# The inverse transforms of one frequency group of a long convolution: twelve split matmuls against four plain fp32 ones and two VectorE operations

## The chip, the cores and the metric

The kernel runs on one core of a Trainium2 chip. The metric is the device time of one execution in microseconds, median of several runs. The engines are named as in the profile: PE (TensorE matmuls), PEld (TensorE weight loads, which overlap PE), DVE (VectorE), ACT (ScalarE), POOL (GpSimd) and SP (SyncE). Each works through its own instructions strictly in the order in which they stand in its program.

## The reference

An encoder layer is applied to two inputs of 1024 rows by 1024 channels. Each is normalised and projected; one part goes through a Fourier branch, another through a Hyena branch, and both are gated, merged and projected again. What matters here is the Hyena branch, which does two long convolutions per channel, one after the other:

```python
def long_conv(u, kf, d):
    L = u.shape[1]
    uf = jnp.fft.rfft(u, n=2 * L, axis=1)
    y = jnp.fft.irfft(uf * kf[None], n=2 * L, axis=1)[:, :L]
    return y + d * u
...
    z = v.astype(jnp.float32)
    for n, gate in enumerate((x1, x2)):
        z = gate.astype(jnp.float32) * long_conv(z, kf[:, n],
                                                 hyena_d[n].astype(jnp.float32))
```

`v`, `x1` and `x2` are three 1024-channel projections of the input after a convolution of width 3; `kf` is the spectrum of filters that the layer computes from small weights.

## The kernel before

All data are fp32. A matmul of full precision is mostly made from values split in two (`split`, L168): ACT rounds the source to a high part of type fp32r, and DVE (or POOL) subtracts it from the source to get the low part. `mm3` (L372) then does three fp32r matmuls: high by high, high by low, low by high. A few matmuls are done once on plain fp32 operands; in the profile such a call of 128x128 shows as two records.

**Phases.** First the Fourier branch; then `phase_main` (L868), which begins with the filters' spectra (written to DRAM as `d_k`) beside some gate projections; then, in `branches` (L911), the convolutions; then the remaining gates, the two output projections and the last one. The tables for the forward transform (`cfw0`, `cfwd`) are loaded at the start of `phase_main`, the inverse table `cinv` in thirds after the filters' iterations 2, 4 and 6 (L903 to L908) by POOL's queue.

**The convolutions.** `branches` goes through 32 of them: 2 batches, in each 8 channel tiles of 128 channels and 2 orders. One step builds the next convolution's front (`conv_front`, L782: the projection `pin`, transpositions `tph`, and the first stages of the transform as sums and differences in `butterfly`), then the present one's back (`conv_back`, L796), then gates it. A projection is 48 matmuls of 128x512 on PE.

**`conv_back`** goes through four groups of frequencies in the order 0, 2, 1, 3 (`GROUPS`, L147). Group 0 is the real one: frequencies with index 0 and 4 modulo 8, whose inputs are real, so its forward transform (`forward`, L593) is four plain fp32 matmuls of 128x128 with `cfw0`. The others take twelve fp32r matmuls with `cfwd`. Then, for every group alike:

- DVE multiplies the spectrum X in PSUM by the filter's (`t`, 1024 wide, L806) and adds the parts to Y (`y`, 512 wide, L810).
- ACT rounds Y to `yh`, DVE makes `yl` (L813). `y` has one buffer, `yh` and `yl` have two each.
- PE does the inverse transforms: twelve fp32r matmuls `pT`, with the parts of Y as the stationary side and `cinv` as the moving one, 256 columns each (L816 to L833). For group 0 the table of frequency index 4 stands there twice, once negated, so that the four quarters of `pT` come out as sums and differences of the two frequency classes already. `pT` is one of two PSUM buffers of the tag "T", which the transpositions `tph` use in turn with it.
- For group 0 ACT copies `pT` to `T0s` (L839), and for group 2 DVE adds and subtracts its `pT` (`U`, and `V` in place of `T0s`). Groups 1 and 3 are combined likewise (`T1s`, `S`, `D`, `ez`). Further sums give the output `yc`.

The program's order is not written by hand: a scheduler places the instructions of each engine by its own estimate of time, and pools with numbered buffers set what must wait. So a change in one place can move instructions elsewhere on the engine.

Of the kernel before, what the change touches and what calls it, by code (L numbers as in the profile page):

```python
# [9 lines left out]
F32 = mybir.dt.float32  # L10
# [6 lines left out]
P = 128  # L17
# [29 lines left out]
def _tables():  # L47
    t = {}
    s = np.arange(P) + 0.5
    fwd, inv = [], []  # L50
    th = np.zeros((P, 8, 6))
    for pi, (f1, hf) in enumerate(PAIRS):
        f = f1 + 8 * (np.arange(P) + P * hf)
        w = 2 * np.pi * f / 2048
        c, sn = np.cos(np.outer(s, w)), np.sin(np.outer(s, w))
        wt = np.full(P, 1 / 1024.0)
        if f1 == 0:
            sn[:, 0] = np.sin(np.pi * s)
            wt[0] = 1 / 2048.0
        fwd += [c, sn]  # L60
        ci, si = (c * wt).T, (sn * wt).T
        if f1 == 0:
            inv += [ci, -si]
        elif f1 == 4:
            inv += [ci, -ci, -si, si]
        else:
            inv += [-si, ci, si]
        ang = w * 127.5
        ct, st = np.cos(ang), np.sin(ang)
        ct2, st2, cm = ct.copy(), st.copy(), ct.copy()  # L70
        if f1 == 0:
            ct2[0], st2[0], cm[0] = 0.0, -1.0, 0.0
        if f1 in (0, 4):
            th[:, pi] = np.stack([ct, -st, -cm, -st, -ct2, st2], axis=1)
        else:
            th[:, pi] = np.stack([ct, -st, 0 * ct, 0 * ct, st, 0 * ct], axis=1)
    t["c_fw0"] = np.concatenate(fwd[:4], axis=1).astype(np.float32)
    t["c_fwd"] = _hl(np.concatenate(fwd[4:], axis=1))
    t["c_inv"] = _hl(np.concatenate(inv, axis=1))
    t["c_th"] = th.astype(np.float32)  # L80


    ta = np.arange(L // 2)
    tp = np.arange(258)
    tabs = []
    for fn in (np.cos, np.sin):
        for r in range(2):
            w = 2 * np.pi * np.outer(2 * np.arange(256) + r, tp) / L
            tabs += [fn(w[0:P]), fn(w[P:2 * P])]
    t["c_seq"] = _hl(np.concatenate(tabs, axis=1))  # L90

    ae = np.zeros((P, 2, 86))
    for b in range(2):
        for r in (0, 2, 32, 34):
            ae[r + b, b] = 1.0 - 2.0 * (tp[:86] % 2)
    t["c_alt"] = ae.astype(np.float32).reshape(P, 2 * 86)
    c = np.arange(P)
    cg = np.cos(2 * np.pi * np.outer(c, c) / 256) / 512
    sg = np.sin(2 * np.pi * np.outer(c, c) / 256) / 512
    sg[0] = 0.0  # L100
    sg[:, 0] = 0.0
    d0 = np.zeros((P, P))
    d0[:, 0] = (1.0 - 2.0 * (c % 2)) / 512
    t["c_chan"] = _hl(np.concatenate([cg, sg, d0], axis=1))
    xs = np.zeros((P, 2, 2, P))
    for g in range(2):
        for r in (g, 32 + g):
            xs[r, 0, g] = (1.0 - 2.0 * (c % 2)) / 512
            xs[r, 1, g, 0] = 1.0 / 512
    t["c_chx"] = xs.astype(np.float32).reshape(P, 4 * P)  # L110


    f32 = np.float32
    pos = np.arange(L, dtype=f32)
    tn = pos / f32(L - 1)
    bands = np.linspace(1e-4, BANDS - 1, BANDS, dtype=f32)
    ang = (f32(2.0 * math.pi) * pos / f32(L))[:, None] * bands[None]
    z = np.concatenate([tn[:, None], np.cos(ang), -np.sin(ang)], axis=-1).astype(f32)
    order = []
    for m in range(4):  # L120
        order.append(256 * m + 128 + np.arange(P))
        order.append(256 * m + 127 - np.arange(P))
    order = np.concatenate(order)
    t["c_z"] = np.ascontiguousarray(z[order].T)
    v = np.zeros((P, 14), f32)
    v[:, 0:8] = -tn[order].reshape(8, P).T
    v[:, 8] = 1.0
    v[127, 8] = 0.0
    v[127, 9] = 1.0
    v[1:, 10] = -1.0  # L130
    v[1:, 11] = 1.0
    v[:, 12] = -1.0
    v[0, 12] = 1.0
    t["c_vec"] = v
    t["c_id"] = np.eye(P, dtype=f32)
    return t
# [5 lines left out]
_o = 0  # L142
for _pi, (_f1, _hf) in enumerate(PAIRS):
    IOFF[_pi] = _o
    _o += 256 if _f1 == 0 else (512 if _f1 == 4 else 384)
INVW = _o
GROUPS = [(0, (0, 1)), (2, (4, 5)), (1, (2, 3)), (3, (6, 7))]  # L147
KOFF = {0: 0, 1: 8, 2: 16, 3: 24}
# [13 lines left out]
class K:  # L162
# [633 lines left out]
    def conv_back(self, n, ct, B, ws):  # L796
        nc = self.nc
        ci = self.cinv
        T = {}
        for g, pairs in GROUPS:  # L800
            X = self.forward(g, pairs, B[g], "pX")
            kt = ws.tile([P, 8, P], F32, tag="k", name="k", bufs=2)
            o = KOFF[g] * P
            nc.sync.dma_start(kt.rearrange("p a b -> p (a b)"), self.d_k[n][ct][:, o:o + 8 * P])
            t = ws.tile([P, 2, 2, 2, P], F32, tag="t1", name="t", bufs=1)
            self.mul("dve", t.rearrange("p k h r c -> p k (h r c)"),  # L806
                     X.rearrange("p h r c -> p (h r c)").unsqueeze(1).to_broadcast([P, 2, 512]),
                     kt.rearrange("p (k a) b -> p k (a b)", k=2))
            Y = ws.tile([P, 2, 2, P], F32, tag="y", name="y", bufs=1)
            self.add("dve", Y, t[:, 0], t[:, 1, :, ::-1])  # L810
            yh = ws.tile([P, 2, 2, P], F32R, tag="yh", name="yh", bufs=2)
            yl = ws.tile([P, 2, 2, P], F32R, tag="yl", name="yl", bufs=2)
            self.split(yh, yl, Y, "dve", "act")  # L813
            Tp = self.psum("T", 2, "pT")
            T4 = Tp.rearrange("p (q c) -> p q c", q=4)
            for r in range(2):  # L816
                for i, pr in enumerate(pairs):
                    w = (yh[:, i, r], yl[:, i, r])
                    o = IOFF[pr]
                    if g == 0:  # L820
                        out = T4[:, r::2]
                        if i == 0:
                            R = [ci[:, hl, o + r * P:o + r * P + P].unsqueeze(1).to_broadcast([P, 2, P]) for hl in range(2)]
                        else:
                            R = [ci[:, hl, o + r * 256:o + r * 256 + 256].rearrange("p (a b) -> p a b", a=2)
                                 for hl in range(2)]
                    elif r == 0:
                        out = T4[:, 0::3]
                        R = [ci[:, hl, o + P:o + 3 * P].rearrange("p (a b) -> p a b", a=2) for hl in range(2)]
                    else:  # L830
                        out = T4[:, 1:3]
                        R = [ci[:, hl, o:o + 2 * P].rearrange("p (a b) -> p a b", a=2) for hl in range(2)]
                    self.ended = self.mm3(out, w, R, i == 0, i == 1)  # L833

            def tt(name):
                return ws.tile([P, 512], F32, tag="tt", name=name, bufs=4)
            if g in (0, 1):
                T[g] = tt(f"T{g}s")
                nc.scalar.copy(T[g], Tp)  # L839
            elif g == 3:  # L840
                S_, D_ = tt("S"), T[1]
                self.add("dve", S_, T[1], Tp)
                self.sub("dve", D_, T[1], Tp)
                ez = ws.tile([P, 2, 256], F32, tag="ez", name="ez", bufs=1)
                self.sub("dve", ez[:, 0], D_[:, 0:256], S_[:, 256:512])
                self.add("dve", ez[:, 1], D_[:, 0:256], S_[:, 256:512])
            else:
                U, V = tt("U"), T[0]
                self.add("dve", U, T[0], Tp)
                self.sub("dve", V, T[0], Tp)  # L850
        q = ws.tile([P, 4, 2, P], F32, tag="q", name="q", bufs=2)
        qf = q.rearrange("p n e s -> p n (e s)")
        self.add("dve", qf[:, 0], U[:, 0:256], S_[:, 0:256])
        self.sub("dve", qf[:, 2], V[:, 0:256], D_[:, 256:512])
        self.stt("dve", qf[:, 1], ez[:, 0], C8, V[:, 256:512])
        self.stt("dve", qf[:, 3], ez[:, 1], -C8, U[:, 256:512])
        y = ws.tile([P, 4, 256], F32, tag="q", name="yc", bufs=2)
        self.add("dve", y[:, :, P:2 * P], q[:, :, 0], q[:, :, 1])
        self.sub("dve", y[:, :, P - 1::-1], q[:, :, 0], q[:, :, 1])
        return y.rearrange("p n s -> p (n s)")  # L860
# [7 lines left out]
    def phase_main(self, nct=8, nb=NB, nf=16):  # L868
        tc, nc, a = self.tc, self.nc, self.a
        with ExitStack() as es:  # L870
# [24 lines left out]
            for i in range(nf):  # L895
# [6 lines left out]
                    self.spill_gate(0, sec, c, ws)  # L902
                if i == 2:  # L903
                    self.cinv = mi.tile([P, 2, INVW], F32R, name="cinv")
                if i in (2, 4, 6):

                    s = slice((2, 4, 6).index(i) * INVW // 3, ((2, 4, 6).index(i) + 1) * INVW // 3)
                    nc.gpsimd.dma_start(self.cinv[:, :, s], a["c_inv"][:, :, s])  # L908
# [560 lines left out]
```

## Time and profile before

| | |
|---|---|
| Median of 3 runs | 2442.94 us (2442.49 to 2445.35) |
| The profiled execution | 2444.67 us |
| Its span, first to last instruction | 2442.9 us |
| Filters and gates ahead of the convolutions | up to about 700 us |
| Convolutions (first and last start of pT) | 731.9 to 1681.3 us |
| PE's mean granted clock | 0.996 |

The profile is of one execution. A line of a group ends in the busy time, the mean duration in ns, and the idle time of the engine ahead of these instructions with what ended it. PE's records overlap: a matmul's record lasts longer than the distance to the next, so what a matmul costs is read from the distance of starts. Tiles are named without buffer numbers; L194 is `mm`, through which nearly all matmuls go, and L181 is `tt`, through which the sums, differences and products on DVE and POOL go, so groups are told apart by their tiles.

### The profile page before, as it was taken

What the parts mean: (1) busy time and instruction counts of PE and PEld (TensorE: products, weight loads), DVE (VectorE), ACT (ScalarE), POOL (GpSimd) and SP (SyncE); (2) the same over time, 40 slices, a digit from 0 to 9 for tenths busy, and PEclk for the clock granted to TensorE, in tenths of its full rate; (3) what the DMA queues carried; (4) which work ended last, traced back from release to release, by engine and by line L of the source; (5) the groups of instructions that cost most, each with busy time, mean ns of one, the idle gap of its engine ahead of it and who ended that gap; (6) DMA issues with size and microseconds to landing.
All of it is one profiled execution on the core that took longest, in us unless ns stands there. A gap on an engine that the chain in (4) does not pass through costs nothing.

```text
span 2442.9 us, 36854 instructions
## 1 busy us (share of the span) xinstructions
PE 2396.8 (98%) x13196; PEld 2084.8 (85%) x13196; DVE 1896.5 (78%) x3405; ACT 1096.7 (45%) x2063; POOL 487.0 (20%) x518
## 2 busy tenths in 40 slices
PE   6999999999999999999999999999999999999998
PEld 5988888888888888888888888888788888888886
DVE  7687888888748999999989999766555455665677
ACT  5546577767633433334223323333344444544343
POOL 1341322222143433331000000112200012122111
PEclk9999999999999999999999999999999999999999
DMA  7535655555555555545444444335454567776543
GB/s 265 187 133 198 218 180 169 169 176 166 172 194 178 172 177 173 163 165 195 147 129 133 141 141 139 121 121 184 141 177 167 190 211 254 253 255 217 170 162 130
DMA packets 225823, 429.36 MB, mean 176 GB/s; under 512 B 23574, under 2 KB 87287, under 8 KB 225256
## 3 DMA queue, kind: packets, MB, share of 16 engines
q1 hardware_dynamic: 198444, 333.34, 42.5%
q0 software_dynamic: 27008, 93.65, 11.1%
q8 instruction: 104, 1.70, 0.3%
q14 instruction: 79, 0.65, 0.1%
q10 hardware_dynamic: 188, 0.02, 0.0%
HBM read 290.60 MB, written 136.31 MB: 175 GB/s over the span
## 4 chain that ended last, share of the span: by engine, by line
PE 92%; DMA 2%; DVE 2%; ACT 1%; issue 1%; POOL 1%; SPq 0%; DVEq 0%; ACTq 0%; POOLq 0%
PE pin L194 41%; PE pT L194 7%; PE pg L194 7%; PE pyf L194 7%; PE pyh L194 7%; PE pX L194 7%; PE po L194 6%; PE pXf L194 3%; PE pfv L194 2%; PE pft L194 1%; PE tph L792 1%; PE tpx L194 1%; DMA x<-in_x 1%; DMA wr<-in_w_fo 0%; DMA d_x<-xg 0%
## 5 line engine op out<-in xcount | busy, mean ns | idle before, releaser
L194 PE MATMUL pin<-xh,wl 128*128 128x512 f32 x1472 | 577.7, 392 | 3.3 <-POOL wl L181 3.3
L194 PE MATMUL pin<-xh,wh 128*128 128x512 f32 x1472 | 577.2, 392 | 0.9 <-DMA wh<-d_w 0.9
L194 PE MATMUL pin<-xl,wh 128*128 128x512 f32 x1472 | 576.2, 392 | 0.4 <-DVE xl L181 0.4
L181 POOL TENSOR_TENSOR wl<-wr,wh 128x512 fp32r<-128x512 f32 x136 | 240.8, 1772 | 1141.9 <-ACT wh L171 1108.1
L171 ACT CAST wh<-wr 128x512 fp32r<-128x512 f32 x264 | 163.5, 620 | 365.0 <-PE pin L194 141.3
L194 PEld LDWEIGHTS pin<-xh,wl 128*128 128x128 f32 x1472 | 277.5, 189 | 55.8 <-POOL wl L181 4.8
L194 PEld LDWEIGHTS pin<-xh,wh 128*128 128x128 f32 x1472 | 277.4, 188 | 52.5 <-DMA wh<-d_w 1.3
L194 PEld LDWEIGHTS pin<-xl,wh 128*128 128x128 f32 x1472 | 277.5, 189 | 52.2 <-DVE xl L181 1.0
L194 PE MATMUL pT<-cinv,yh 128*128 128x256 f32 x1024 | 193.1, 283 | 0.0
L194 PEld LDWEIGHTS pT<-cinv,yh 128*128 128x128 f32 x1024 | 164.0, 190 | 9.0
L181 DVE TENSOR_TENSOR t<-pX,k 128x1024 f32<-128x1024 f32 x128 | 155.7, 1216 | 11.0 <-PE pX L194 9.3
L181 DVE TENSOR_TENSOR wl<-wr,wh 128x512 fp32r<-128x512 f32 x128 | 87.8, 687 | 94.1 <-ACT wh L171 93.8
L194 PE MATMUL pX<-bh,cfwd 128*128 128x256 f32 x768 | 159.6, 286 | 0.0
L194 PE MATMUL pyf<-sf,wh 128*128 128x512 f32 x512 | 157.7, 389 | 0.0
L194 PE MATMUL pyh<-sh,wh 128*128 128x512 f32 x512 | 157.3, 389 | 0.0
L171 ACT CAST bh<-b 128x512 fp32r<-128x512 f32 x144 | 89.0, 620 | 126.0 <-DVE b L181 84.2
L194 PE MATMUL pT<-cinv,yl 128*128 128x256 f32 x512 | 144.9, 283 | 0.0
L171 ACT CAST yh<-y 128x512 fp32r<-128x512 f32 x128 | 79.2, 618 | 112.3 <-DVE y L181 89.5
L194 PEld LDWEIGHTS pX<-bh,cfwd 128*128 128x128 f32 x768 | 126.4, 190 | 2.5
L194 PEld LDWEIGHTS pyh<-sh,wh 128*128 128x128 f32 x512 | 96.1, 188 | 19.9
L194 PEld LDWEIGHTS pyf<-sf,wh 128*128 128x128 f32 x512 | 96.1, 188 | 19.9
L194 PE MATMUL pX<-bl,cfwd 128*128 128x256 f32 x384 | 109.6, 285 | 0.0
(354 smaller groups left out, 5262.9 us busy)
## 6 DMA issues: line engine op xcount, KB each, us to landing
k<-d_k SPq DMA_DIRECT2D x128, 512.0 KB, 4.0
wr<-in_w_in SPq DMA_DIRECT2D x136, 256.0 KB, 3.1
d_g<-gt SPq DMA_DIRECT2D x124, 256.0 KB, 2.8
d_k<-kt SPq DMA_DIRECT2D x128, 128.0 KB, 2.1
d_k<-kt SPq DMA_DIRECT2D x64, 256.0 KB, 2.3
wr<-in_w_fo POOLq DMA_DIRECT2D x64, 256.0 KB, 4.1
g<-d_g SPq DMA_DIRECT2D x64, 256.0 KB, 4.4
wr<-in_w_ho POOLq DMA_DIRECT2D x64, 256.0 KB, 4.0
```

Of the source, the lines that this page charges most:

```text
L171: self.rounded = nc.scalar.copy(h, src)
L181: return e.tensor_tensor(out, a, b, op=op)
L194: return self.nc.tensor.matmul(out, lhsT, rhs, start=start, stop=stop, skip_group_check=shared)
L792: nc.tensor.transpose(tp[:, q * P:(q + 1) * P], eo[:, e, q], self.ident)
```

## The change

Group 0 alone is treated in a way of its own. The inverse tables of its two frequency classes leave `c_inv` (which shrinks from 3072 to 2304 columns per part) and form a table `c_in0` of 512 fp32 columns: cosine and negative sine of class 0, then of class 4, each once. It is loaded by SP's queue after the filters' iteration 2. In `conv_back`, Y of group 0 is not split: it goes unrounded into four plain fp32 matmuls of 128x128, one per class and part, whose results fill the four quarters of a PSUM buffer `pT0`. ACT copies the right half (class 4) to the right half of `T0s`; DVE adds the left half of `pT0` and that copy into the left half of `T0s`, then puts their difference into the right half. Y of group 0 lies in one of the two `yl` buffers and not in the single `y` one. From group 2 on all is as before.

```diff
@@ _tables
-        if f1 == 0:
-            inv += [ci, -si]
-        elif f1 == 4:
-            inv += [ci, -ci, -si, si]
+        if f1 in (0, 4):
+            in0 += [ci, -si]
         else:
             inv += [-si, ci, si]
...
+    t["c_in0"] = np.concatenate(in0, axis=1).astype(np.float32)
...
@@ offsets in c_inv
-    _o += 256 if _f1 == 0 else (512 if _f1 == 4 else 384)
+    _o += 0 if _f1 in (0, 4) else 384
...
@@ conv_back
-            Y = ws.tile([P, 2, 2, P], F32, tag="y", name="y", bufs=1)
+            Y = ws.tile([P, 2, 2, P], F32, tag="y" if g else "yl", name="y" if g else "y0", bufs=1 if g else 2)
             self.add("dve", Y, t[:, 0], t[:, 1, :, ::-1])
+            if g == 0:
+
+                Tp = self.psum("T", 2, "pT0")
+                for i in range(2):
+                    for r in range(2):
+                        s = slice((2 * i + r) * P, (2 * i + r + 1) * P)
+                        self.mm(Tp[:, s], Y[:, i, r], self.cin0[:, s], True, True)
+                T[0] = ws.tile([P, 512], F32, tag="tt", name="T0s", bufs=4)
+                lo, hi = T[0][:, 0:256], T[0][:, 256:512]
+                nc.scalar.copy(hi, Tp[:, 256:512])
+                self.add("dve", lo, Tp[:, 0:256], hi)
+                self.sub("dve", hi, Tp[:, 0:256], hi)
+                continue
...
-                    if g == 0:
-                        out = T4[:, r::2]
-                        if i == 0:
-                            R = [ci[:, hl, o + r * P:o + r * P + P].unsqueeze(1).to_broadcast([P, 2, P]) for hl in range(2)]
-                        else:
-                            R = [ci[:, hl, o + r * 256:o + r * 256 + 256].rearrange("p (a b) -> p a b", a=2)
-                                 for hl in range(2)]
-                    elif r == 0:
+                    if r == 0:
...
-            if g in (0, 1):
-                T[g] = tt(f"T{g}s")
+            if g == 1:
+                T[g] = tt("T1s")
                 nc.scalar.copy(T[g], Tp)
...
@@ phase_main
                     self.cinv = mi.tile([P, 2, INVW], F32R, name="cinv")
+                    self.cin0 = mi.tile([P, 4 * P], F32, name="cin0")
+                    nc.sync.dma_start(self.cin0, a["c_in0"])
```

More of the change, by code (lines that the diff above doesn't have):

```diff
@@ L49, in _tables @@
     s = np.arange(P) + 0.5
-    fwd, inv = [], []
+    fwd, in0, inv = [], [], []
     th = np.zeros((P, 8, 6))
```

## The prediction

> **What bounds the kernel now.** I read the page first, then the stretches of the convolutions, then who waits for whom, then the chain of work, the timeline and the groups. From the page:
>
> ```profile
> PE 2396.8 (98%) x13196; PEld 2084.8 (85%) x13196; DVE 1896.5 (78%) x3405; ACT 1096.7 (45%) x2063; POOL 487.0 (20%) x518
> ...
> PE 92%; DMA 2%; DVE 2%; ACT 1%; issue 1%; POOL 1%; SPq 0%; DVEq 0%; ACTq 0%; POOLq 0%
> PE pin L194 41%; PE pT L194 7%; PE pg L194 7%; PE pyf L194 7%; PE pyh L194 7%; PE pX L194 7%; PE po L194 6%; PE pXf L194 3%; PE pfv L194 2%; PE pft L194 1%; PE tph L792 1%; PE tpx L194 1%; DMA x<-in_x 1%; DMA wr<-in_w_fo 0%; DMA d_x<-xg 0%
> ...
> L194 PE MATMUL pT<-cinv,yh 128*128 128x256 f32 x1024 | 193.1, 283 | 0.0
> ...
> L194 PE MATMUL pT<-cinv,yl 128*128 128x256 f32 x512 | 144.9, 283 | 0.0
> ```
>
> PE is busy for 98% and makes 92% of the chain that ends last; pT, which the change cuts, is 7% of that chain. The 1536 records of pT are 32 convolutions (2 batches, 8 channel tiles, 2 orders) by 4 groups by 12. None of them sat idle (0.0 behind the last bar). Since a busy PE need not be the bound, I look at the stage where these matmuls stand, stretch by stretch (columns: busy us of PE, PEld, DVE, ACT, POOL, each with its count, then PE's granted clock, DMA share and GB/s):
>
> ```profile
> 800.00:900.00 100.00, 100.00 (x608) 89.21 (x607) 98.56 (x151) 38.63 (x70) 36.58 (x36) 1.00 0.54 173
> 900.00:1000.00 100.00, 100.00 (x610) 89.42 (x609) 96.82 (x156) 36.46 (x66) 35.15 (x35) 1.00 0.53 171
> 1000.00:1100.00 100.00, 100.00 (x612) 89.46 (x612) 95.53 (x146) 39.94 (x73) 36.71 (x35) 1.00 0.50 165
> ...
> 1300.00:1400.00 100.00, 100.00 (x606) 89.22 (x605) 94.97 (x157) 31.13 (x56) 0.00 (x0) 1.00 0.45 143
> ...
> 1700.00:1800.00 100.00, 97.01 (x420) 79.48 (x419) 56.52 (x64) 39.67 (x59) 17.60 (x14) 0.98 0.47 157
> ```
>
> and at all that PE waited for from 690 to 1700 us:
>
> ```profile
> PE pin L194 <- DMA wh<-d_w: 0.9, 1, 0.9
> PE pin L194 <- DVE xl L181: 0.4, 1, 0.4
> ```
>
> PE never pauses for a pT, pX or transposition: it is the bound there, at the full clock. The second thing to see is DVE at 95.5 to 98.6% of the first batch's stretches and 95% of the second's: it is the next bound, with 9.1 us free in 300 (300 less 98.56, 96.82 and 95.53). So PE's saving counts in full only as far as DVE can follow.
>
> **PE's part of the change.** Removed per convolution: the twelve fp32r matmuls of the first group. Added: four fp32 ones of 128x128. Starts and not durations give the cost, since matmuls overlap. From the chain of work (start, us, what), then from the timeline, where eight records of the forward transform of the same group are followed by pT, and from the groups:
>
> ```profile
> 720.12 0.88 PE tph L792 x8
> ...
> 737.22 1.44 PE pT L194 x12
> ...
> 755.22 13.63 PE pin L194 x60
> ```
>
> ```profile
> 1005.58 0.98 PEld L194 LDWEIGHTS pX<-b,cfw 128*128 128x128 f32 x8
> ...
> 1006.48 0.30 PEld L194 LDWEIGHTS pT<-cinv,yh 128*128 128x128 f32 x2
> ```
>
> ```profile
> L194 PE MATMUL pX<-b,cfw 128*128 128x128 f32 x256 | 34.8, 274 | 0.0
> ...
> L194 PE MATMUL tpx<-dg,xk 128*128 128x128 f32 x128 | 15.6, 276 | 1.4 <-ACT xg L344 0.9 <-DMA xk<-in_x 0.5
> ```
>
> Twelve pT take 1.44 us, 0.12 each (a pin matmul takes 13.63/60 = 0.227). The forward transform calls four fp32 matmuls of exactly the new shape per convolution, 128 in all, and has 256 records: one call is two records. Eight records take 1006.48 - 1005.58 = 0.90 us of weight loads. In the forward transform the table is the stationary side and the data moves; here it is the other way round. tpx, with its data stationary, has 128 records for 64 calls and the same 276 ns, so the roles do not matter. Saving: 1.44 - 0.90 = 0.54 us per convolution, times 32 = **17.3 us**. The ends: were the eight records as long as their durations (274 ns each, 2.19 us), the convolution would lose 0.75 us; at the group's busy time (34.8/32 = 1.09 us) it would gain 0.35. I take 0.54, as the 0.90 us are a stream with other work on both sides.
>
> [...] In the trace the two kinds load alike, 191 and 190 ns:
>
> ```profile
> L194 PEld LDWEIGHTS pT<-cinv,yh 128*128 128x128 f32 x1024 | 164.0, 190 | 9.0
> ...
> L194 PEld LDWEIGHTS pX<-b,cfw 128*128 128x128 f32 x256 | 33.4, 191 | 1.6
> ```
>
> **DVE's part.** Removed: the subtraction that makes yl for the first group, 512 wide. Added: a sum and a difference, 256 wide each, one operand in PSUM. From the groups by tile (min/median/max in ns), and the timeline:
>
> ```profile
> L171 ACT CAST yh<-y x128: 603/621/627, 729.3 to 1675.7; 128x512 fp32r<-128x512 f32 x128
> L181 DVE TENSOR_TENSOR yl<-y,yh x128: 672/681/1672, 732.8 to 1676.3; 128x512 fp32r<-128x512 f32 x128
> ```
>
> ```profile
> L839 ACT COPY T0s<-pT x32: 578/586/591, 738.9 to 1670.8; 128x512 f32<-128x512 f32 x32
> L181 DVE TENSOR_TENSOR U<-T0s,pT x32: 671/677/689, 740.2 to 1675.5; 128x512 f32<-128x512 f32 x32
> L181 DVE TENSOR_TENSOR q<-U,S x32: 410/418/1069, 755.1 to 1683.2; 128x256 f32<-128x256 f32 x32
> ```
>
> ```profile
> 1000.71 0.75 DVE L181 TENSOR_TENSOR b<-bs 128x256 f32<-128x256 f32 x2
> ...
> 1001.38 0.68 DVE L181 TENSOR_TENSOR y<-t 128x512 f32<-128x512 f32 x1
> ...
> 1007.75 0.68 DVE L181 TENSOR_TENSOR yl<-y,yh 128x512 fp32r<-128x512 f32 x1
> ...
> 1010.56 0.28 PE L194 MATMUL pT<-cinv,yl 128*128 128x256 f32 x1
> ...
> 1010.68 1.28 DVE L181 TENSOR_TENSOR bl<-b,bh 128x512 fp32r<-128x512 f32 x2
> ...
> 1011.88 0.68 DVE L181 TENSOR_TENSOR y<-t 128x512 f32<-128x512 f32 x1
> ```
>
> A PSUM operand costs nothing extra (677 beside 681). In a stream a 256 takes (1001.38 - 1000.71)/2 = 0.335 us and a 512 (1011.88 - 1010.68)/2 = 0.60. So DVE gets 2 x 0.335 - 0.60 = +0.07 us per convolution; without overlap, 2 x 0.418 - 0.60 = +0.24. I take 0.07. DVE's 9.1 us in 300 are 3.0%; a convolution of the first batch takes some 28.2 us (half of the 32.7 us of three projections, 144 x 0.227, plus 48 pT and 36 pX at 0.12, 8 fp32 records and 8 transpositions at 0.11), so DVE has 0.86 us free in each. PE's 0.54 and DVE's 0.07 leave 0.25 us: DVE goes to 99%, but stays below PE. It runs ahead, too: the yl that ends at 1008.43 is used at 1010.56, 2.1 us later.
>
> [...]
>
> **ACT** loses the cast (0.62) and has 256 columns to copy in place of 512; at 39% it is covered. **DMA**: c_inv shrinks by a quarter, c_in0 adds one load of 256 KB on SP's queue during the filters; before the first pT nothing else moves in the program's order.
>
> ```profile
> wr<-in_w_in SPq DMA_DIRECT2D x136, 256.0 KB, 3.1
> ```
>
> A load of that size lands in 3.1 us, hundreds of us before its use: nothing.
>
> **The new waits.** The sum on DVE waits for PE's four matmuls and ACT's copy, and while it waits, everything behind it on DVE waits, with PE behind that. The first group's Y now also lies in the ring of two yl buffers: the yl two further on must wait until the four matmuls have read it. I laid the built program's order beside the paces above. In 28 of 32 convolutions DVE has, between the product of the second group (which releases PE's later transforms) and its first instruction that needs pT0, 4.0 to 7.4 us more work than PE has up to pT0's end; in two it has 2.4 and 0.7 us more, in two (the first ones of the batches) PE has 0.5 and 1.6 us more. So the waits are covered but for about 2 us. The PSUM ring of two: pT0 is held until the difference is done, not just until a copy; up to its next user PE has 6.4 us of other work or more. I cost the waits at 2 us.
>
> **Sum.** The profiled execution took 2444.67 us (span 2442.9). 2444.67 - 17.3 + 2 = 2429.4; the median of the runs is 1.7 us lower, so **2427.6 us**.
>
> **Rivals.**
>
> *DVE becomes the bound.* For it: 95 to 99% busy, in order, and some of its operations already take far longer than their median (yl up to 1672 ns). Against it: its idle time is mostly waiting for PE, which now comes earlier. If DVE can't get below its 0.86 us of idle time, the dozen dense convolutions of the first batch gain nothing and lose the 0.07, and of the second batch half the gain is lost: 17.3 - 12 x 0.61 - 16 x 0.27 = 5.7 us gained; 2437. If only the first batch suffers: 2433.
>
> *The wait for pT0 stops DVE.* Slower than before. Two waits of this kind exist:
>
> ```profile
> DVE S L181 <- PE pT L194: 33.3, 15, 5.8
> ...
> ACT T0s L839 <- PE pT L194: 31.8, 14, 4.4
> ```
>
> They come at about every second convolution, 2.2 us each. The new sum is DVE's version of the second: if DVE stood 2.2 us there in each convolution, behind its 0.25 us of spare time, PE would get its operands 2 us late each time and lose 32 x (2.2 - 0.25 - 0.54) = 45 us net; at every second one, 32 x (1.1 - 0.25 - 0.54) = 10: 2453. It decides from 0.8 us of wait per convolution. Against it: the order above gives DVE 4 us of other work.
>
> *The fp32 matmuls do not run at 0.11 a record.* At the 274 ns of their durations: 2443 + 24 = 2467. Nearly excluded by the 0.90 us.
>
> **Chances.** The forecast (2421 to 2431) 0.62; DVE bound (2431 to 2441) 0.22; DVE stopped by pT0 0.12; fp32 dearer, or order shifts that eat the gain, 0.04. The lower end allows for the 3 us of PE's pauses between 1700 and 1800 us, which may fall otherwise: 2427.6 - 2 (no wait for pT0 at all) - 3 = 2422.6, and 1.6 more for the scatter of the runs (2442.49 to 2445.35). The range 2421 to 2441 leaves out the last two cases and a little below. A measurement of this kernel tells about 0.2% (4.9 us) from no change: faster by more (below 2438) 0.80, within 0.07, slower 0.13.
>
> **What would show it.** PE's group pT falls to 1152 records, pT0 has 256 with no idle time, and eight of its records take 0.9 us. DVE's share between 800 and 1100 us rises to 98 to 99%. If DVE takes over, PE waits for yl, bl or t appear that are absent now; if pT0 stops DVE, there is a wait of the sum for ACT's copy, or of yl for pT0, over 25 us in total. The forecast is wrong if PE's busy share in the convolutions falls below 99%, or if the end shifts without PE's work having shrunk by 17 us.

## The result and the profile after

The changed kernel takes 2427.14 us (median of five runs, 2425.10 to 2428.06) against 2442.94 us (2442.40 to 2445.35): a ratio of 0.9931 with a 95% interval of 0.9918 to 0.9945. The profiled execution took 2428.06 us, its span is 2426.1 us.

First the engines' totals, from the page of the changed kernel, then its matmuls that write pT and what follows them (the view of the tile pT: min/median/max in ns, first and last start):

```profile
PE 2379.7 (98%) x13068; PEld 2066.0 (85%) x13068; DVE 1905.1 (79%) x3437; ACT 1070.9 (44%) x2031; POOL 497.9 (21%) x518
```

```profile
L193 PE MATMUL pT<-cinv,yh x768: 274/283/365, 735.3 to 1667.3; 128*128 128x256 f32 x192
...
L193 PE MATMUL pT<-cinv,yl x384: 274/283/388, 737.0 to 1667.5; 128*128 128x256 f32 x192
...
L193 PE MATMUL pT<-cin,y x256: 270/275/275, 729.5 to 1653.9; 128*128 128x128 f32 x128
L180 DVE TENSOR_TENSOR T0s<-pT,T0s x64: 401/414/424, 731.4 to 1655.1; 128x256 f32<-128x256 f32 x64
```

PE has 13068 records in place of 13196: 384 of pT went (768 + 384 = 1152 are left of 1536) and 256 came, and PE is busy 2396.8 - 2379.7 = 17.1 us less. The span fell by 16.8. So nearly all of PE's saving reached the end.

One of the new groups of eight records, in the timeline of PE:

```profile
932.66 1.05 PE L193 MATMUL pT<-cin,y 128*128 128x128 f32 x8
933.47 0.48 PE L193 MATMUL pT<-cinv,yh 128*128 128x256 f32 x2
933.79 0.28 PE L193 MATMUL pT<-cinv,yl 128*128 128x256 f32 x1
```

From the first of the eight to the next matmul it is 933.47 - 932.66 = 0.81 us; the two yh behind them take 0.32 where two take 0.24 in a stream, so the eight cost 0.81 + 0.08 = 0.89.

The stretches of the convolutions and their end, before and after (columns as in the prediction: busy us and count of PE, PEld, DVE, ACT, POOL, then PE's granted clock, DMA share, GB/s):

```profile
800.00:1100.00 300.00, 300.00 (x1826) 268.09 (x1825) 290.91 (x451) 115.03 (x208) 108.44 (x106) 1.00 0.53 170
1100.00:1200.00 100.00, 98.70 (x568) 85.89 (x567) 93.41 (x144) 36.07 (x58) 7.28 (x4) 1.00 0.51 165
1200.00:1500.00 300.00, 300.00 (x1820) 268.07 (x1820) 277.29 (x449) 91.58 (x162) 0.00 (x0) 1.00 0.44 141
```

```profile
800.00:1100.00 300.00, 298.06 (x1800) 265.11 (x1800) 299.21 (x462) 105.84 (x195) 118.44 (x104) 1.00 0.53 172
1100.00:1200.00 100.00, 98.52 (x551) 85.39 (x550) 88.87 (x144) 33.74 (x55) 9.48 (x4) 0.98 0.51 169
1200.00:1500.00 300.00, 300.00 (x1802) 266.92 (x1802) 276.95 (x458) 83.40 (x151) 0.00 (x0) 1.00 0.44 141
1700.00:1800.00 100.00, 99.01 (x435) 81.25 (x434) 57.92 (x72) 42.05 (x65) 13.24 (x13) 1.00 0.47 161
```

Two things are to be seen. In the first batch's dense stretch DVE is now busy for 299.21 of 300 us, and PE, which never paused there, pauses 1.94 us. And the stretch 1700 to 1800, where PE had 97.01 us and a clock of 0.98, now has 99.01 and 1.00. What PE waited for from 690 to 1700 us, sorted by total (us in total, times, longest):

```profile
PE tph L791 <- DVE T0s L180: 1.2, 2, 0.7
PE pin L193 <- DVE xl L180: 1.0, 1, 1.0
PE pX L193 <- DVE bl L180: 0.6, 1, 0.6
PE pin L193 <- DMA wh<-d_w: 0.2, 1, 0.2
PE pX L193 <- DVE t L180: 0.2, 1, 0.2
```

The new waits are small (tph waits for the PSUM buffer that the difference gives back), 3.2 us in all where there were 1.3. The waits for bl and t, 0.8 us together, are of the kind that the prediction set as a sign of DVE taking over. And from DVE's waits in the same stretch:

```profile
DVE T0s L180 <- ACT T0s L819: 1.9, 2, 1.5
```

The new sum waits for ACT's copy in two of 32 convolutions, for 1.9 us together.

### The profile page after: what moved, and what is told of

The parts are those of the page before. It is cut to its first block, busy times and chain, and to the rows that moved or that the text cites. A ratio compares the mean times of both kernels' runs of the same rounds, so it can differ in the third digit from the quotient of the medians.

```text
span 2426.1 us, 36569 instructions
## 1 busy us (share of the span) xinstructions
PE 2379.7 (98%) x13068; PEld 2066.0 (85%) x13068; DVE 1905.1 (79%) x3437; ACT 1070.9 (44%) x2031; POOL 497.9 (21%) x518
## 4 chain that ended last, share of the span: by engine, by line
PE 48%; DMA 2%; DVE 1%; issue 1%; ACT 0%; POOL 0%; SPq 0%; DVEq 0%; ACTq 0%; POOLq 0%
PE pin L193 14%; PE pyh L193 7%; PE pg L193 7%; PE po L193 6%; PE pyf L193 6%; PE pT L193 4%; PE pX L193 4%; DMA wr<-in_w_fo 1%; DMA xraw<-d_x 1%; PE tph L791 1%; DVE xsum L180 0%; DMA wr<-in_w_in 0%; DMA wraw<-in_w_in 0%; DVE wl L180 0%; DVE xsum L176 0%
## 5 line engine op out<-in xcount | busy, mean ns | idle before, releaser
L180 POOL TENSOR_TENSOR wl<-wr,wh 128x512 fp32r<-128x512 f32 x136 | 254.1, 1869 | 1133.7 <-ACT wh L170 1100.4
L193 PE MATMUL pT<-cinv,yh 128*128 128x256 f32 x768 | 145.6, 284 | 0.0
L193 PEld LDWEIGHTS pT<-cinv,yh 128*128 128x128 f32 x768 | 123.1, 190 | 6.6
L170 ACT CAST yh<-y 128x512 fp32r<-128x512 f32 x96 | 59.5, 619 | 144.7 <-DVE y L180 136.9
L180 DVE TENSOR_TENSOR bl<-b,bh 128x512 fp32r<-128x512 f32 x144 | 104.2, 727 | 7.0 <-ACT bh L170 6.7
```

What stands on the lines that cost most here:

```text
L170: self.rounded = nc.scalar.copy(h, src)
L180: return e.tensor_tensor(out, a, b, op=op)
L193: return self.nc.tensor.matmul(out, lhsT, rhs, start=start, stop=stop, skip_group_check=shared)
```

## The experiments

Two theories stand against each other. **PE**: the gain is PE's own, 17 us of matmuls less, and what DVE and ACT have less or more hardly counts. **DVE**: the gain (or a good part of what is missing in it) is set by DVE, or ACT's relief; then a change of DVE's load moves the end and one of PE's doesn't. A third question is what the buffer of the unsplit Y does.

All changes are against the changed kernel unless another is named. The runs of the kernel before beside them had medians of 2442.70 us (double_table, no_sums, split_once, more_dve), 2441.72 (before_more_dve, one_wide, y_ring, after_again) and 2441.90 (own_y, two_y, before_yl, wide_own).

### PE's work changed alone

**double_table.** Still fp32 and still once, but the table of class 4 stands there twice, once negated, as it did before; the sums come out of PE, and DVE has neither split nor sums for group 0.

```diff
-            in0 += [ci, -si]
+            in0 += [ci, -si] if f1 == 0 else [ci, -ci, -si, si]
...
-                for i in range(2):
-                    for r in range(2):
-                        s = slice((2 * i + r) * P, (2 * i + r + 1) * P)
-                        self.mm(Tp[:, s], Y[:, i, r], self.cin0[:, s], True, True)
+                T4, c0 = Tp.rearrange("p (q c) -> p q c", q=4), self.cin0
+                for r in range(2):
+                    one = c0[:, r * P:(r + 1) * P].unsqueeze(1).to_broadcast([P, 2, P])
+                    two = c0[:, (2 + 2 * r) * P:(4 + 2 * r) * P].rearrange("p (a b) -> p a b", a=2)
+                    self.mm(T4[:, r::2], Y[:, 0, r], one, True, False)
+                    self.mm(T4[:, r::2], Y[:, 1, r], two, False, True)
...
-                nc.scalar.copy(hi, Tp[:, 256:512])
-                self.add("dve", lo, Tp[:, 0:256], hi)
-                self.sub("dve", hi, Tp[:, 0:256], hi)
+                nc.scalar.copy(T[0], Tp)
...
-                    self.cin0 = mi.tile([P, 4 * P], F32, name="cin0")
+                    self.cin0 = mi.tile([P, 6 * P], F32, name="cin0")
```

> The four fp32 matmuls get 256 columns each (class 4's table twice, once negated) and accumulate the sums and differences in PSUM; ACT copies all 512, DVE makes no sum. Against the kernel before, DVE and ACT are relieved more than by the change (DVE by 0.60 us per convolution), PE gets eight records of twice the width: some 1.76 us if a record's time doubles, against 1.44. If PE's time is what was saved: slower than before, about 2443 + 32 x 0.32 = 2453. If the relief of DVE and ACT, or the shorter way without a split, was the gain: 2427 or less.

Measured: 2454.80 us (2454.05 to 2455.76), ratio 1.0053 (1.0038 to 1.0068). Its eight records of 256 columns, by the weight loads in the timeline, and its dense stretch:

```profile
929.99 1.71 PEld L193 LDWEIGHTS pT<-cin,y 128*128 128x128 f32 x8
931.72 0.41 PEld L193 LDWEIGHTS pT<-cinv,yh 128*128 128x128 f32 x2
```

```profile
800.00:1100.00 300.00, 296.15 (x1721) 261.53 (x1720) 291.33 (x429) 105.26 (x189) 100.14 (x102) 1.00 0.52 166
1200.00:1500.00 300.00, 300.00 (x1766) 266.13 (x1765) 266.76 (x430) 86.28 (x149) 0.00 (x0) 1.00 0.43 137
```

Eight records take 1.73 us, 0.216 each: 1.73 - 1.44 = 0.29 us more than the twelve of before, 9.3 us in 32 convolutions. DVE has less to do than in either kernel (266.76 of 300 in the second batch, where before had 277.29), and the kernel is 12.1 us slower than before. The DVE theory, by which it should have been at least as fast as the changed one, falls. The remaining 2.8 us are of the size of PE's pauses (3.85 us in the first row), which come here although DVE has 8.7 us to spare.

**split_once.** The own table and the sums on DVE stay, but Y is split again and each product is made of three fp32r matmuls, twelve of 128x128.

```diff
-    t["c_in0"] = np.concatenate(in0, axis=1).astype(np.float32)
+    t["c_in0"] = _hl(np.concatenate(in0, axis=1))
...
-            Y = ws.tile([P, 2, 2, P], F32, tag="y" if g else "yl", name="y" if g else "y0", bufs=1 if g else 2)
+            Y = ws.tile([P, 2, 2, P], F32, tag="y", name="y" if g else "y0", bufs=1)
...
+                yh = ws.tile([P, 2, 2, P], F32R, tag="yh", name="yh", bufs=2)
+                yl = ws.tile([P, 2, 2, P], F32R, tag="yl", name="yl", bufs=2)
+                self.split(yh, yl, Y, "dve", "act")
...
-                        self.mm(Tp[:, s], Y[:, i, r], self.cin0[:, s], True, True)
+                        self.mm3(Tp[:, s], (yh[:, i, r], yl[:, i, r]), (self.cin0[:, 0, s], self.cin0[:, 1, s]), True, True)
...
-                    self.cin0 = mi.tile([P, 4 * P], F32, name="cin0")
-                    nc.sync.dma_start(self.cin0, a["c_in0"])
+                    self.cin0 = mi.tile([P, 2, 4 * P], F32R, name="cin0")
+                    nc.gpsimd.dma_start(self.cin0, a["c_in0"])
```

> The own table and DVE's sums stay, but Y is split and each transform is three fp32r matmuls of 128 columns, twelve per convolution. It takes the one half of the change (once each, sums on DVE) without the other (plain fp32). If a record's pace is set by the weight load (0.11 to 0.12 us whatever the width), PE saves 0 to 0.12 us per convolution and DVE has 0.67 more than before, more than PE leaves it: 2440 to 2452. If halving the width is the gain: about 2430.

Measured: 2448.79 us (2447.73 to 2450.25), ratio 1.0028 (1.0016 to 1.0040). Two of its weight loads, nine loads apart, and the stretch of the change of batch:

```profile
1224.26 0.19 PEld L193 LDWEIGHTS pT<-cin,yl 128*128 128x128 f32 x1
...
1225.27 0.19 PEld L193 LDWEIGHTS pT<-cin,yl 128*128 128x128 f32 x1
```

```profile
1100.00:1200.00 100.00, 93.31 (x524) 81.02 (x523) 89.06 (x134) 33.37 (x53) 6.68 (x4) 0.97 0.48 163
```

An fp32r record of 128 columns takes 1.01/9 = 0.112 us, hardly less than one of 256 (0.12): halving the columns saves some 12 x 0.008 = 0.1 us per convolution, 3 us in all. DVE has both the split and the sums, and PE pauses 6.69 us at the change of batch. So neither half of the change pays by itself: fp32 with the doubled table costs 12 us, the single table with three products 6 us. Only together do they come to eight records of 128 columns.

**no_sums.** The sum and the difference are left out (the output isn't the transform's); ACT copies all of pT0.

```diff
-                nc.scalar.copy(hi, Tp[:, 256:512])
-                self.add("dve", lo, Tp[:, 0:256], hi)
-                self.sub("dve", hi, Tp[:, 0:256], hi)
+                nc.scalar.copy(T[0], Tp)
```

> Leaves out the sum and the difference of group 0 (ACT copies the four quarters as they are), so the result is not the reference's. PE's work is that of the changed kernel, DVE has 0.67 us less per convolution. If PE is the bound and DVE only brushes it: the few us of waits that PE has in the changed kernel's convolutions go, 2422 to 2425. If DVE has become the bound: in the dozen dense convolutions of the first batch 0.67 each or more, 2419 or less; all through, 2427 - 21 = 2406.

Measured: 2422.27 us (2421.28 to 2424.79), ratio 0.9923 (0.9907 to 0.9940). Its dense stretch:

```profile
800.00:1100.00 300.00, 299.50 (x1804) 265.92 (x1804) 296.68 (x446) 109.97 (x197) 110.79 (x105) 1.00 0.53 169
```

32 x 2 x 0.335 = 21 us of DVE's work is gone, and the end comes 4.9 us earlier than that of the changed kernel, or 2 us by the two ratios (0.9931 - 0.9923 of 2443), whose intervals overlap. PE's pauses in the stretch fall from 1.94 to 0.50 us. All that DVE's sums cost is therefore a few us.

Put beside double_table, this run separates PE from DVE. The two give DVE and ACT the same operations (ACT copies all of pT0, DVE has neither split nor sums for group 0) in another order, and the eight records of PE have 128 columns here and 256 there. The times are 2422.27 and 2454.80 us, 32.5 apart, and the records' pace makes 32 x (1.73 - 0.89) = 26.9 of them.

### How near DVE is to its limit

**more_dve** adds one operation per convolution that changes nothing that is used later: 512 wide, into pT0, behind the difference. **before_more_dve** puts the same operation into the kernel before.

```diff
                 self.sub("dve", hi, Tp[:, 0:256], hi)
+                self.add("dve", Tp, Tp, T[0])
```

```diff
@@ the kernel before
                 nc.scalar.copy(T[g], Tp)
+                if g == 0:
+                    self.add("dve", Tp, Tp, T[0])
```

> The changed kernel with one more DVE operation per convolution, 512 wide (0.6 us), that adds the finished T0s to the dead PSUM buffer. In the changed kernel's trace DVE is busy 99.6 to 100% from 800 to 1100 us. If DVE is at its limit there: 0.6 us for each of some 12 to 15 convolutions, 2434 to 2438, and more if the second batch reaches the limit as well. If it still had room behind its lead of some us: 2427 to 2429.

> The kernel before with the same additional DVE operation of 0.6 us per convolution. If PE was the bound with 0.86 us of DVE's time free per convolution, most of it fits: 2443 to 2448. If DVE was the bound already: 2443 + 32 x 0.6 = 2462.

Measured: more_dve 2436.44 us (2432.65 to 2439.93), ratio 0.9978 (0.9969 to 0.9987); before_more_dve 2452.03 us (2450.68 to 2454.96), ratio 1.0041 (1.0027 to 1.0054). Their stretches, more_dve first:

```profile
800.00:1100.00 300.00, 295.95 (x1768) 262.39 (x1767) 299.68 (x459) 105.77 (x192) 107.75 (x105) 0.99 0.52 167
1100.00:1200.00 100.00, 93.15 (x516) 80.39 (x515) 86.25 (x134) 30.92 (x48) 5.98 (x3) 0.96 0.48 161
1200.00:1500.00 300.00, 300.00 (x1793) 266.98 (x1792) 277.73 (x461) 83.79 (x153) 0.00 (x0) 1.00 0.44 142
```

```profile
800.00:1100.00 300.00, 298.28 (x1788) 263.67 (x1786) 297.50 (x447) 110.99 (x199) 108.89 (x104) 1.00 0.52 167
1100.00:1200.00 100.00, 94.72 (x539) 82.73 (x540) 91.82 (x144) 37.35 (x62) 8.43 (x5) 0.98 0.50 169
```

The operation takes 0.60 us in a stream, 19.2 us in 32. The changed kernel loses 9.3 to 9.9 us by it (against its medians of 2427.14 and 2426.55), as expected if DVE was at its limit. The kernel before loses 10.3, which is outside of both expectations for it: neither is it covered by the 3% that DVE has free, nor does it count in full. It is lost in the first batch and at the change of batch (PE 298.28 of 300 and 94.72 of 100, where it had 300.00 and 98.70); in more_dve likewise, while its second batch, with DVE at 277.73, loses nothing. So the 3% that DVE had free in the dense stretch of the kernel before did not take up the added work. Two of PE's waits in more_dve, from 690 to 1740 us, limit what its loss says of DVE's time:

```profile
PE pin L193 <- DMA wh<-d_w: 4.1, 2, 3.0
...
PE pT L193 <- DVE pT L180: 1.8, 1, 1.8
```

The largest wait is for weights that a DMA brings, at the change of batch, and the added operation also holds the buffer of pT0 longer, for which PE waits once. How much of the 9.3 to 9.9 us comes by DVE's time alone isn't separated.

**one_wide** makes both results by one DVE operation of 512 in place of two of 256, with a second copy (negated) on ACT; DVE has 0.07 us less per convolution, as in the kernel before.

```diff
-                nc.scalar.copy(hi, Tp[:, 256:512])
-                self.add("dve", lo, Tp[:, 0:256], hi)
-                self.sub("dve", hi, Tp[:, 0:256], hi)
+                nc.scalar.copy(lo, Tp[:, 256:512])
+                nc.scalar.mul(hi, Tp[:, 256:512], -1.0)
+                both = T[0].rearrange("p (a b) -> p a b", a=2)
+                self.add("dve", both, Tp[:, 0:256].unsqueeze(1).to_broadcast([P, 2, 256]), both)
```

> The changed kernel with one DVE operation of 512 in place of two of 256: ACT copies the class 4 half and its negative side by side, DVE adds the class 0 half to both. DVE has 0.07 us less per convolution, ACT some 0.35 more. If DVE brushes the bound: 1 to 2 us faster, 2425 to 2427; if only PE counts: 2427.

Measured: 2424.57 us (2421.11 to 2426.48), ratio 0.9927 (0.9914 to 0.9941), beside **after_again**, the changed kernel once more in the same set:

> The changed kernel itself, beside the others on one chip: 2427, with 2425 to 2428.

with 2426.55 us (2422.99 to 2427.91), ratio 0.9931 (0.9919 to 0.9944). The 2 us between them are of the size of the sum's 32 x 0.07, but lie inside the intervals.

### The buffer of the unsplit Y

**y_ring** puts Y of group 0 back into the single buffer of the tag "y"; **two_y** does so too, but gives this tag two buffers; **own_y** gives Y of group 0 a buffer of its own; **before_yl** is the kernel before with only the line of the buffer taken from the change.

```diff
@@ y_ring
-            Y = ws.tile([P, 2, 2, P], F32, tag="y" if g else "yl", name="y" if g else "y0", bufs=1 if g else 2)
+            Y = ws.tile([P, 2, 2, P], F32, tag="y", name="y" if g else "y0", bufs=1)
@@ two_y (and bufs=2 at the other two users of the tag)
+            Y = ws.tile([P, 2, 2, P], F32, tag="y", name="y" if g else "y0", bufs=2)
@@ own_y
+            Y = ws.tile([P, 2, 2, P], F32, tag="y" if g else "y0", name="y" if g else "y0", bufs=1)
@@ before_yl, in the kernel before
-            Y = ws.tile([P, 2, 2, P], F32, tag="y", name="y", bufs=1)
+            Y = ws.tile([P, 2, 2, P], F32, tag="y" if g else "yl", name="y" if g else "y0", bufs=1 if g else 2)
```

> The changed kernel with Y of group 0 in the single y buffer, as before, and not in one of the two yl buffers. The sum of the second group must then wait until the four matmuls have read Y. If DVE's lead covers such waits: within 2 us of 2427, which also shows what a mere change of order does. If waits for pT0 stop DVE: 5 us or more slower.

Measured: 2462.02 us (2461.15 to 2466.19), ratio 1.0083 (1.0070 to 1.0097): 35 us over the changed kernel in the same set. That is on the side of the second expectation (5 us or more), but far beyond what it named. The largest of PE's waits from 690 to 1740 us, and its stretches:

```profile
PE pT L193 <- ACT yh L170: 14.1, 7, 3.5
```

```profile
800.00:1100.00 300.00, 295.42 (x1727) 261.09 (x1727) 283.97 (x430) 102.37 (x183) 102.61 (x105) 0.98 0.52 167
1200.00:1500.00 300.00, 285.86 (x1655) 251.98 (x1655) 264.71 (x438) 80.45 (x143) 0.00 (x0) 0.97 0.41 131
```

PE pauses 4.58 and 14.14 us in stretches where the changed kernel had 1.94 and none, and its clock falls to 0.98 and 0.97 there. DVE is less busy, not more (283.97 where it was 299.21), so it isn't short of time there. One of the pauses, in the timeline:

```profile
1395.91 1.27 DVE L176 SCALAR_TENSOR_TENSOR x<-pin,wsh,x 128x1023 f32<-128x1023 f32 x1
1396.03 0.28 PE L193 MATMUL pT<-cinv,yl 128*128 128x256 f32 x1
...
1398.44 0.69 DVE L180 TENSOR_TENSOR y<-t 128x512 f32<-128x512 f32 x1
...
1399.16 0.62 ACT L170 CAST yh<-y 128x512 fp32r<-128x512 f32 x1
...
1399.83 0.80 PE L193 MATMUL pT<-cinv,yh 128*128 128x256 f32 x2 [3.52 <-ACT yh L170]
```

PE has finished one group's transforms and stands still until the next group's Y is made and cast; DVE makes this Y behind the width-3 convolutions of the projections (v and x) and sums (b) of the next convolution.

> The changed kernel with all Ys in one tag that has two buffers and not one. If the 35 us of the single y buffer came from the second group's sum waiting until the four fp32 matmuls had read Y: they go with the second buffer, 2424 to 2430. If they came from the order that the scheduler chose, or from Y's place: 2440 or more.

Measured: 2427.05 us (2426.38 to 2428.24), ratio 0.9941 (0.9925 to 0.9956). In both batches:

```profile
800.00:1100.00 300.00, 295.42 (x1769) 261.90 (x1769) 298.53 (x457) 105.12 (x194) 112.38 (x104) 0.99 0.51 166
...
1200.00:1500.00 300.00, 300.00 (x1809) 267.38 (x1808) 280.34 (x468) 85.53 (x153) 0.00 (x0) 1.00 0.44 143
```

The second buffer takes the 35 us away. So the single buffer is their cause: Y of group 0, which nothing copies any more, holds it until PE's four matmuls have read it, and the Ys of the later groups need it. By which way it costs, an actual wait or the order that the scheduler builds around the buffer, isn't separated: DVE's waits of y for pT come to only 2.0 us in y_ring, and at the place shown it is the order that has Y late.

> The changed kernel with Y of group 0 in a buffer of its own, shared with no yl. If sharing the yl ring costs the waits that I priced at 2 us: 2424 to 2426. If they are covered: 2426 to 2428.

Measured: 2434.20 us (2431.34 to 2436.70), ratio 0.9970 (0.9958 to 0.9982): 7 us slower than two_y in the same set, which is as fast as the changed kernel, where no difference was expected. Its dense stretch, and the largest of PE's waits from 690 to 1700 us:

```profile
800.00:1100.00 300.00, 294.16 (x1761) 261.22 (x1760) 299.48 (x456) 106.05 (x195) 116.65 (x104) 0.99 0.52 166
```

```profile
PE tph L791 <- DVE T0s L180: 2.4, 2, 1.8
```

It has the operations of the changed kernel and one buffer more; its order on the engines is another. PE pauses 5.84 us in the dense stretch in place of 1.94. But two_y pauses 4.58 us there (300 less 295.42) and is as fast as the changed kernel, so the dense stretch alone doesn't explain the 7 us.

> The kernel before with one line of the change alone: Y of group 0 lies in a yl buffer, but is split and transformed as before. There ACT and DVE free it and PE does not read it, so nothing should be gained: 2440 to 2446. If the ring is what brought the gain: about 2430.

Measured: 2443.81 us (2440.79 to 2448.70), ratio 1.0009 (1.0000 to 1.0018). The move to the other buffers gains nothing by itself. Three of its stretches matter, since it computes just what the kernel before does:

```profile
800.00:1100.00 300.00, 300.00 (x1822) 268.03 (x1821) 297.23 (x454) 115.70 (x208) 113.89 (x104) 1.00 0.54 170
1100.00:1200.00 100.00, 97.98 (x556) 84.78 (x555) 93.46 (x144) 35.22 (x58) 6.54 (x4) 0.98 0.49 164
...
1700.00:1800.00 100.00, 99.11 (x437) 81.77 (x436) 56.81 (x68) 40.70 (x61) 15.74 (x14) 1.00 0.49 164
```

DVE has 297.23 where before had 290.91, with PE at 300.00 in both: the busy share of a fixed stretch moves by 2% with one buffer's place and the order that the scheduler builds on it. At the change of batch PE pauses 2.02 us with a clock of 0.98, where before had 1.30 and 1.00. And the pause of PE behind 1700 us is shorter here (0.89 us, clock 1.00). Both come without the rest of the change.

**wide_own** joins one_wide and own_y:

```diff
-            Y = ws.tile([P, 2, 2, P], F32, tag="y" if g else "yl", name="y" if g else "y0", bufs=1 if g else 2)
+            Y = ws.tile([P, 2, 2, P], F32, tag="y" if g else "y0", name="y" if g else "y0", bufs=1)
...
+                nc.scalar.copy(lo, Tp[:, 256:512])
+                nc.scalar.mul(hi, Tp[:, 256:512], -1.0)
... (as in one_wide)
```

> The changed kernel with one wide DVE operation and Y of group 0 in its own buffer. If DVE's time in the first batch is what is left between the kernel and PE's bound: at or a little below the 2424.6 of the one wide operation, 2421 to 2425; if both only reorder: 2425 to 2428.

Measured: 2428.77 us (2423.18 to 2429.61), ratio 0.9944 (0.9931 to 0.9956). The gain hoped for isn't there. No version that computes the transform was clearly faster than the changed kernel.

## Why the prediction was right, step by step

**What bounds the kernel** held. double_table decides it: with DVE lighter and PE heavier the kernel became slower than before, and no_sums, with 21 us of DVE's work gone, gained a few us only. Of the 32.5 us between these two, whose operations on DVE and ACT are the same, 26.9 are the pace of PE's eight records.

**PE's term** held: 17.3 us were predicted, 17.1 us of busy time went, and eight records take 0.89 us where 0.90 was taken from pX. The records' durations (275 ns in the median) say nothing of this, as foreseen. Between fp32 and fp32r no difference of pace shows at this width: the eight fp32 records take 0.89/8 = 0.111 us each, an fp32r record of 128 columns in split_once 0.112 us.

**DVE's term** (+0.07 us) is consistent with one_wide, which takes it away and stands 2 us lower, but that is inside the intervals. The forecast that DVE would go to 98 to 99% held roughly: 299.21 of 300, 99.7%. But before_yl shows that this share moves with one buffer's place too, so it is weak evidence of a limit. The sign of DVE taking over, waits of PE for yl, bl or t, came as well, with only 0.8 us in two places. An operand in PSUM cost DVE nothing extra, as the prediction had it: 414 ns in the median for the new sums beside 418 for the sum q of the same width, which has none of its operands in PSUM.

**The waits** were costed too low. The term was 2 us, with all of it at the wait for pT0. On DVE that wait is 1.9 us for the sum; on PE, which sets the end, only 1.2 us go with pT0's buffer (tph). By the rows above, the convolutions cost more: in the changed kernel 1.94 us of pauses from 800 to 1100, 1.48 from 1100 to 1200 and, at a clock of 0.98, another 2; before it were none, 1.30 and none. That is 5.4 against 1.3 us, so about 4 us: 2 of longer pauses, the size of the term, and 2 of the slower clock, which the sum didn't have. In the dense stretch, the step that was too kind is "DVE goes to 99%, but stays below PE": on the mean it does, at single places it doesn't, and PE waits there for T0s and bl. The other half, at the change of batch, can't be put down to DVE's added work, since before_yl has it as well (2.02 us of pauses at 0.98). Of the 19.2 us that more_dve and before_more_dve add to DVE, about half comes through (9.3 and 10.3 us).

**What made up for it** stood outside the sum. From 1700 to 1800 us, the kernel before lost 2.99 us in pauses and 2 by its clock of 0.98, the changed one 0.99 and nothing: 4 us gained, which the prediction had only in the lower end of its range. So 17.3 gained, 4 lost and 4 gained make 17.3. By the first starts of tph and pg, from 697.0 to 1741.5 us before and from 694.9 to 1722.2 after, this part of the kernel shrank by 17.2 us. The profiled executions differ by 2444.67 - 2428.06 = 16.6, as the changed one was 2.1 us ahead when this part began and lost about 2.5 behind it; why is open. That the two errors cancel is luck. before_yl has the worse change of batch and the better end as well, so neither needs the cheaper matmuls; that they come from the order is argued, not shown.

**The rivals.** DVE as the bound of the whole gain is refuted by double_table; in part it limits the kernel, and by before_more_dve it did so from the start. The wait for pT0 that stops DVE, priced at 2453, didn't come: DVE's sum waited for 1.9 us in all. The other wait that the prediction named, for Y's buffer, is cheap in the ring of two that the change uses, as it said, but the choice of that ring matters more than any term of the sum: with the single buffer the kernel takes 2462.02 us, more than before the change.

**What stays open**: why own_y, with more buffers, is 7 us slower. It pauses 5.84 us in the dense stretch, but two_y pauses 4.58 there without being slower; that the 7 us come from its order was not tested by an order held fixed.

## What to carry to other kernels

Compare a matmul written once in fp32 with its three-product form by records times columns, with distances measured in a stream: here fp32 pays at 128 columns (eight records, 0.90 us, against twelve of 256, 1.44 us) and loses at 256 (1.73 us). When a value is no longer copied or split but read by TensorE as it is, its buffer is held until TensorE comes to it, so don't let it share a single buffer with the values behind it: here that cost 35 us, and a ring of two cost nothing. And where a second engine has only 3% to spare beside the one that bounds, don't count added work on it as free (here about half of 19.2 us came through), and expect a moved buffer, which also changes the scheduler's order, to move the time by several us (own_y is 7 us slower than two_y), which limits how finely a sum can be checked.

## What the runs showed of the hardware

A short pause of PE cost twice in the two places shown here: for 3 to 5 us behind it, matmuls ran at about half pace. In y_ring, behind the pause of 3.52 us shown above (starts of 512-wide matmuls):

```profile
1400.98 0.63 PE L193 MATMUL pin<-xl,wh 128*128 128x512 f32 x1
1401.41 0.63 PE L193 MATMUL pin<-xh,wl 128*128 128x512 f32 x1
```

In the kernel before, behind a pause of 1.93 us:

```profile
1729.30 0.50 PE L194 MATMUL pin<-xh,wl 128*128 128x512 f32 x1 [1.93 <-POOL wl L181]
...
1729.87 0.40 PE L194 MATMUL pin<-xl,wh 128*128 128x512 f32 x1
1730.10 0.39 PE L194 MATMUL pin<-xh,wl 128*128 128x512 f32 x1
...
1730.70 0.63 PE L194 MATMUL pin<-xl,wh 128*128 128x512 f32 x1
1731.12 0.63 PE L194 MATMUL pin<-xh,wl 128*128 128x512 f32 x1
...
1733.97 0.40 PE L194 MATMUL pin<-xh,wh 128*128 128x512 f32 x1
1734.21 0.40 PE L194 MATMUL pin<-xl,wh 128*128 128x512 f32 x1
```

The distance is 0.43 in the first, and goes from 0.23 to 0.42 and back to 0.24 in the second. In before the slow part begins 1 us after PE has resumed and lasts some 3 us; the granted clock is 0.51 from 1730.3 to 1733.6 us. Not every pause is followed by this: from 1100 to 1200 us, pauses of 1.30 us in sum left the clock of the kernel before at 1.00, and 1.48 us in the changed kernel came with 0.98. By an estimate from its stretches, most of y_ring's 35 us come about in this way: pauses of 18.7 us in the 600 us shown, and a clock of 0.98 and 0.97 there, which is about 300 x 0.02 + 300 x 0.03 = 15 us more.
